# Two-layer RG-LRU and forgetting-attention trunk: splits of y later and spread, low parts of weights on VectorE, single banks for the end blocks

## The chip, the core and the metric

The kernel runs on one core of a Trainium2 chip. A core has five engines that each work through their own queue in order: TensorE (PE in the profile, with its weight loads as PEld), VectorE (DVE), ScalarE (ACT), GpSimd (POOL) and SyncE (SP), which here issues the DMA transfers. The metric is the time of one execution on the device in microseconds.

## The reference, cut to what matters

One batch of 1024 tokens by 1024 channels, two layers, float32. Layer 1 in the list is a recurrence; layer 2 is causal attention with 16 heads of 64, a forget gate in the logits, and a SiLU gate on its output.

```python
def fox_mixer(h, w_in, b_f, w_out):
    u = h @ w_in                                  # q, k, v, gate, forget logits
    cum = jnp.cumsum(jax.nn.log_sigmoid(f_logit), axis=1)
    # for each block of 128 queries:
    logits = jnp.einsum("bqhd,bkhd->bhqk", q_blk, kf) * scale
    logits = logits + (cq_blk[..., :, None] - ck[:, :, None, :])
    logits = jnp.where(mask[None, None], logits, NEG_INF)
    p = jax.nn.softmax(logits, axis=-1)
    o = jnp.einsum("bhqk,bkhd->bqhd", p, vf)
    y = o * jax.nn.silu(gate)
    return y @ w_out

def reference(x, ...):
    for i in range(DEPTH):                        # 2
        h = rms_norm(x, norm_g[i])
        x = x + (lru_mixer if i % 2 == 0 else fox_mixer)(h, ...)
    return rms_norm(x, final_g)
```

## The kernel before

Every float32 operand of a matmul is split into a high part, cast by ScalarE (`to_hi`), and a low part, the operand less the high one (`to_lo`). A product is three matmuls: high by high, high by low, low by high. For weights, `split_weights` loads `wf`, casts `wh` on the engine `hi_eng` and subtracts `wl` on `lo_eng`; `weights` does so for four (or fewer) 128x128 blocks at a time.

The first layer fills the time to about 440 us, the second the rest. In the second, x is held transposed, channels on the partitions, in two halves `c` of 512 tokens, with the residual in DRAM (`x1d`). Heads go in pairs. For a head, `maxima` makes the scores S of each 128 queries, masks them and finds their maxima on VectorE and takes the exponentials p (and their sums) on ScalarE; `weigh` transposes p on TensorE, splits it into `ph` and `pl` and multiplies by the values into O, which goes to `yo`. At the end of a head's `maxima` the sums are turned to reciprocals, transposed on TensorE (`tr`), copied (`rc`) and sent through DRAM (`recd`, `recb`) so that they lie along the rows. `scale` multiplies the gate `sg` by `recb` on GpSimd, `gated` multiplies `yo` by that, also on GpSimd. For pairs 0 to 5 the result goes to DRAM (`y1d`); for pairs 6 and 7 `split_y` splits it into `yhh` and `yhl`, which stay in SBUF.

`run` walks a string of digits and dots: a digit advances a step of the attention, a dot takes one step of the generator `fill`, which gives TensorE work between. Up to head 11, `fill` projects the next pair's keys and queries (`kq_units`) and gate (`g_units`). From head 12 on it also holds `load_y` and `split_loaded` (y of pairs 0 to 5, six splits for each half), `partial` (the output projection over those six pairs, for blocks `db` of 128 channels and both halves, added to `x1d`) and `turned` for the first half. `turned` is an end block: it transposes the residual x into PSUM, adds the products of pairs 6 and 7, squares for the norm's sum (ScalarE) and multiplies by the norm's gains (`res`, VectorE). After the last head the first half's four results are scaled and stored, and `turned` runs for the second half. The values of four heads are projected by `values(g)`, g = 0 to 3.

The program's text doesn't set the order of each engine's queue alone: a scheduler that simulates the program's time line reorders instructions. `issue_after` ties a step to the matmul before it.

Of the kernel before, what the change touches and what calls it, by code (L numbers as in the profile page):

```python
# [38 lines left out]
def trunk(ctx: ExitStack, tc: tile.TileContext, xt, w0, wg, wo0, pc, gn, gf, w1, wv, wf, bf, wo1, out):  # L39
# [431 lines left out]
    with ExitStack() as l1:  # L471
# [30 lines left out]
        def values(g):  # L502
# [3 lines left out]
            for k in range(0, KT, 2):  # L506
                src = [(wv[g, :, k : k + 2], slice(0, 256))]
                if ex:
                    src.append((wf[:, k : k + 2], slice(256, 256 + ex)))
                parts += split_weights(src, (2, 256 + ex), nc.scalar, nc.gpsimd)  # L510
            Vs[2 * g], Vs[2 * g + 1] = [], []
# [32 lines left out]
        kqw = {}  # L544

        def kq_units(pair, parts=((1, (0, 1)), (0, (0, 1)))):

            for is_k, hs in parts:
# [4 lines left out]
                if hs[0] == 0 or pair == 0:  # L553
                    kqw[is_k] = list(weights(w1[is_k * 8 + pair]))
                hi, lo = kq[pair, is_k]
# [70 lines left out]
        first = values(0)  # L626
        for _ in range(9):
            next(first)
# [5 lines left out]
        def g_units(pair, hs=(0, 1)):  # L634

            if hs[0] == 0:
                sgs[pair] = at.tile([P, SEQ], F32, tag="sg", name="sg1")
                gw[0] = list(weights(w1[16 + pair]))
            sg = sgs[pair]

            def use(h, pt):
                g_ = sg[:, h * HALF : (h + 1) * HALF]
                nc.scalar.activation(g_, pt, AF.Tanh, scale=0.5)
                nc.vector.scalar_tensor_tensor(g_, g_, 1.0, pt, ALU.add, ALU.mult)

            yield from project(gw[0], use, hs)
# [107 lines left out]
        def gated(hd, c, sub=slice(0, HALF)):  # L754

            if hd % 2 == 0:
                return
            pair = hd // 2
            yo = yos[pair, c][:, sub]
            nc.gpsimd.tensor_tensor(  # L760
                yo, yo, sgs[pair][:, c * HALF + sub.start : c * HALF + sub.stop], ALU.mult
            )
            if hd >= 13:
                split_y(c, pair, yo, sub)
            else:
                nc.sync.dma_start(y1d[c, pair], yo)
# [47 lines left out]

# [11 lines left out]
        def residual(c, q):  # L826
            xs = [wpool.tile([P, 2, 256], F32, tag=("wh", "wl")[q], name="x1") for d in range(4)]
            for d, x in enumerate(xs):
                nc.sync.dma_start(x, x1d[c, :, 2 * d : 2 * d + 2, q * 256 : (q + 1) * 256])
            return xs  # L830

        def turned(c, q):
# [11 lines left out]
            for b in range(2):  # L844
                cs = slice(q * 256 + b * P, q * 256 + (b + 1) * P)
                ss = ssq[c][:, 4 * q + 2 * b : 4 * q + 2 * b + 2]
                for h, hs in enumerate(halves):
                    if c == 1 and b == 1:
                        if h == 0:
                            two = two_banks("turn")  # L850
                        pt = two[:, h]
                    else:
                        pt = ps.tile([P, HALF], F32, tag="gO"[c * q], name="turn")

                    for i in range(4):
                        x = xs[2 * h + i // 2][:, i % 2, b * P : (b + 1) * P]
                        matmul(pt[:, i * P : (i + 1) * P], x, ident, start=i == 0, stop=False, is_transpose=True)
# [59 lines left out]
        for hd in range(HEADS):  # L917
            pair = hd // 2
            if hd % 2 == 0:
                if hd < 12:  # L920
                    fill = kq_units(pair + 1, ((1, (0, 1)), (0, (0,))))
                elif hd == 12:
                    rest = [(db, c) for db in range(2, KT) for c in range(2)]
                    fill = chain(
                        kq_units(7),
                        g_units(7, (0,)),
                        load_y(0),
                        g_units(7, (1,)),
                        load_y(1),
                        split_loaded(0),  # L930
                        partial([(0, 0), (1, 0)]),
                        split_loaded(1),
                        partial([(0, 1), (1, 1)] + rest),
                        turned(0, 0),
# [6 lines left out]
            if hd == HEADS - 1:  # L941
                break
            scale(hd)
            gated(hd, 0)
            side = late() if hd == 14 else iter(())
            run(second, weigh(hd, 1), maxima(hd + 1, 0), fill=fill, side=side)
            drain(side)
            gated(hd, 1)
            if hd < 12:
                drain(fill)  # L950
            if hd % 4 == 3 and hd < 12:
                drain(values(hd // 4 + 1))
            if hd + 2 < HEADS:
# [13 lines left out]
        for q in range(2):  # L967
            left[1, q] = residual(1, q)
        r = root_mean(ssq[0])
        for i, o in enumerate(first_half):  # L970
            nc.vector.tensor_scalar(o, o, r[:, i : i + 1], None, ALU.mult)
            nc.sync.dma_start(out[i], o)
        run("." * 18, fill=chain(turned(1, 0), turned(1, 1)))


# [57 lines left out]
```

## Time and profile before

| | |
|---|---|
| runs, us | 1153.79, 1154.62, 1159.84 (median 1154.62) |
| profiled execution, us | 1156.08 |
| its span, us | 1154.1 |
| mean granted TensorE clock | 0.992 |
| busy TensorE, VectorE, ScalarE, GpSimd, us | 1121.8, 723.0, 593.2, 230.1 |
| low parts of weights on GpSimd | 114 instructions, 166.2 us |

Times in the views are counted from the start of the span. A row of a timeline gives start, duration, engine (SPq is SyncE's queue issuing a transfer), line, operation and tiles, out<-in, and in brackets how long the engine was idle before and what released it. A row of the chain of waits gives start, duration and what ran. A row of the waits gives who waited for whom, the total, the number of times and the longest. A row of the windows gives the length, then for each of TensorE, its weight loads, VectorE, ScalarE and GpSimd the busy time and number of instructions, then the granted TensorE clock, the share of the DMA engines and GB/s.

### The profile page before, as it was taken

Reading aid. Unit: us, or ns where it says so; the run is one execution under the profiler, and the core shown is the slowest. Engines: PE = TensorE matmul, PEld = TensorE weight load, DVE = VectorE, ACT = ScalarE, POOL = GpSimd, SP = SyncE. Lnnn points to the kernel's source line nnn. Section 1 sums busy time; section 2 is a strip of 40 time slices with the busy share of each in tenths; the row PEclk is TensorE's granted clock in tenths of the full one; section 3 lists DMA queues with packets and bytes.
Section 4 is the critical chain, followed back from the end, with each engine's and each line's share of the span. In section 5 each row is a group of like instructions: output and inputs, shape, how many; then the busy total and the mean of one; then the engine's idle time right before and its main releaser. Section 6 shows DMA issues by size and latency. Waiting matters only on the chain.

```text
span 1154.1 us, 15825 instructions
## 1 busy us (share of the span) xinstructions
PE 1121.8 (97%) x5713; PEld 942.8 (82%) x5713; DVE 723.0 (63%) x1222; ACT 593.2 (51%) x1081; POOL 230.1 (20%) x159
## 2 busy tenths in 40 slices
PE   9999999999999999999999999999999999979996
PEld 7788888888888887978888988889888898858874
DVE  7589766777567789566665356663666535746644
ACT  8388345355553657455555355554555534534434
POOL 1212112211121102342222122222232221011010
PEclk9999999999999999999999999999999999989999
DMA  6111111111111124353434135241352512835444
GB/s 212 51 41 51 46 56 52 41 55 41 51 55 40 56 64 157 88 134 88 120 84 107 46 88 124 79 119 45 77 129 74 129 44 67 237 104 160 130 128 182
DMA packets 63637, 105.42 MB, mean 91 GB/s; under 512 B 9444, under 2 KB 24420, under 8 KB 63560
## 3 DMA queue, kind: packets, MB, share of 16 engines
q1 hardware_dynamic: 63560, 104.42, 31.6%
q8 instruction: 45, 0.74, 0.3%
q14 instruction: 32, 0.26, 0.1%
HBM read 63.30 MB, written 15.93 MB: 69 GB/s over the span
## 4 chain that ended last, share of the span: by engine, by line
PE 86%; DVE 4%; issue 3%; DMA 3%; POOL 2%; ACT 2%; SPq 0%; POOLq 0%; ACTq 0%; DVEq 0%
PE gps L54 31%; PE ops L54 16%; PE ups L54 11%; PE vps L54 6%; PE S L54 6%; PE O L54 5%; PE pt L58 5%; PE gate L54 3%; PE turn L54 2%; DMA recb<-recd 1%; POOL sg L705 1%; POOL wl L96 1%; DMA recd<-rc 1%; DVE sq L162 1%; DVE hl L238 1%
## 5 line engine op out<-in xcount | busy, mean ns | idle before, releaser
L96 POOL TENSOR_TENSOR wl<-wf,wh 128x512 fp32r<-128x512 f32 (+1 forms) x114 | 166.2, 1463 | 664.3 <-ACT wh L85 472.2
L54 PE MATMUL gps<-hh,wh 128*128 128x512 f32 x576 | 228.9, 398 | 0.2 <-DVE qkl L565 0.2
L54 PE MATMUL gps<-hh,wl 128*128 128x512 f32 x576 | 226.7, 394 | 0.1
L54 PE MATMUL gps<-hl,wh 128*128 128x512 f32 x576 | 226.7, 393 | 0.0
L678 ACT ACTIVATE p<-S,m 128x128 f32<-128x128 f32 (+7 forms) x128 | 94.8, 741 | 141.1 <-DVE m L673 139.7
L85 ACT CAST wh<-wf 128x512 fp32r<-128x512 f32 (+2 forms) x156 | 94.4, 607 | 141.1 <-PE ops L54 41.9
L96 DVE TENSOR_TENSOR pl<-pt,ph 128x512 fp32r<-128x512 f32 (+1 forms) x198 | 98.8, 541 | 101.6 <-ACT ph L85 101.1
L54 PEld LDWEIGHTS gps<-hl,wh 128*128 128x128 f32 x576 | 108.2, 188 | 24.5
L54 PEld LDWEIGHTS gps<-hh,wl 128*128 128x128 f32 x576 | 108.7, 189 | 20.4 <-POOL wl L96 0.6
L54 PEld LDWEIGHTS gps<-hh,wh 128*128 128x128 f32 x576 | 108.5, 188 | 20.0 <-DVE qkl L565 0.4
L673 DVE CUSTOM_DVE_ANT_0 S<-S,mask 128x128 f32<-128x128 f32 (+7 forms) x128 | 97.4, 762 | 40.5 <-PE S L54 39.0
L85 ACT CAST ph<-pt 128x512 fp32r<-128x512 f32 (+1 forms) x198 | 83.0, 474 | 28.9 <-PE pt L58 23.5
L54 PE MATMUL S<-T,U 96*128 96x512 f32 (+7 forms) x384 | 92.1, 349 | 0.0
L361 DVE TENSOR_TENSOR x<-x,ops 128x512 f32<-128x512 f32 x80 | 54.1, 682 | 50.9 <-PE ops L54 50.8
L58 PE MATMUL pt<-ident,p 128*128 128x128 f32 x576 | 80.0, 275 | 0.0
L54 PEld LDWEIGHTS S<-T,U 128*128 128x128 f32 (+1 forms) x384 | 69.1, 190 | 13.2 <-ACT p L678 0.8
L54 PE MATMUL ups<-hh,wh 128*128 128x512 f32 x192 | 76.7, 400 | 2.5 <-DVE us L271 1.9
L58 PEld LDWEIGHTS pt<-ident,p 128*128 128x128 f32 x576 | 69.2, 142 | 10.7 <-issue 0.4
L54 PE MATMUL ups<-hl,wh 128*128 128x512 f32 x192 | 76.5, 398 | 0.2
L54 PE MATMUL ops<-yh,wh 128*128 128x512 f32 x192 | 76.1, 396 | 0.5 <-DVE x L453 0.5
L54 PE MATMUL vps<-wl,hh 128*128 128x256 f32 (+1 forms) x256 | 72.8, 286 | 3.7 <-POOL wl L96 3.7
L54 PE MATMUL ups<-hh,wl 128*128 128x512 f32 x192 | 76.0, 396 | 0.0
(176 smaller groups left out, 2184.3 us busy)
## 6 DMA issues: line engine op xcount, KB each, us to landing
wf<-in_w SPq DMA_DIRECT2D x100, 256.0 KB
wf<-in_wo SPq DMA_DIRECT2D x64, 128.0 KB
U<-qkh SPq DMA_DIRECT2D x64, 128.0 KB
T<-qkh SPq DMA_DIRECT2D x28, 256.0 KB
x<-in_xt SPq DMA_DIRECT2D x16, 256.0 KB
x1d<-x SPq DMA_DIRECT2D x16, 256.0 KB
wf<-in_wv SPq DMA_DIRECT2D x16, 256.0 KB
U<-qkl SPq DMA_DIRECT2D x32, 128.0 KB
```

What stands on the lines that cost most here:

```text
L54: pe[0] = nc.tensor.matmul(*args, **kw)
L58: pe[0] = nc.tensor.transpose(*args)
L85: nc.scalar.copy(hi, src)
L96: return eng.tensor_tensor(lo, src, f32(hi), ALU.subtract)
L162: eng.tensor_tensor(parts[0], parts[0], sq, ALU.add)
L238: nc.vector.scalar_tensor_tensor(lo, x, g_, f32(hi), ALU.mult, ALU.subtract)
L361: nc.vector.tensor_tensor(x, x, pt, ALU.add)
L673: nc.vector.tensor_tensor_reduce(S[:, :n], S[:, :n], mask[:, SEQ - n :], -1.0, -NEG, ALU.add, ALU.min, accum_out=m)
L678: seen[0] = nc.scalar.activation(p, S[:, :n], AF.Exp, bias=m, scale=-1.0, accum_out=sums[:, i : i + 1])
L705: nc.gpsimd.tensor_tensor(sg, sg, recs[hd // 2][rows, cs], ALU.mult)
```

## The change

Six things are edited.

1. `values` takes its low parts on VectorE for g = 1 to 3 (g = 0, which also carries the forget logits' columns, keeps GpSimd), and after its first two weight tiles it yields; the main loop takes that first step ahead of the second `run` of the head before.
2. `kq_units` and `g_units` of pairs 1 to 7 take their low parts on VectorE; pair 0 stays on GpSimd.
3. The split of y for pair 6 is called later in the program: half 0 after head 13's second `run`, half 1 after head 14's first, and no longer within `gated`.
4. `split_loaded` yields after every second pair, and `beside` takes its steps between steps of the gate projection and of `partial`, where they came as six at once. The weights of `partial` are split a block ahead (`split_out`).
5. `partial` goes two channel blocks at a time for each half. `residual` for the first quarter loads eight tiles of one block each; the others load as before, with the two tags exchanged.
6. `turned` takes one PSUM bank for each block of results, and the first half's four scalings and stores come from a generator, `finish`, that runs beside the last end blocks.

```diff
@@ values
-                parts += split_weights(src, (2, 256 + ex), nc.scalar, nc.gpsimd)
+                parts += split_weights(src, (2, 256 + ex), nc.scalar, nc.gpsimd if ex else nc.vector)
+                if k == 2:
+                    yield
@@ kq_units, g_units
+        def low(pair):
+            return nc.vector if pair else nc.gpsimd
...
-                    kqw[is_k] = list(weights(w1[is_k * 8 + pair]))
+                    kqw[is_k] = list(weights(w1[is_k * 8 + pair], lo_eng=low(pair)))
...
-                gw[0] = list(weights(w1[16 + pair]))
+                gw[0] = list(weights(w1[16 + pair], lo_eng=low(pair)))
@@ gated
-            if hd >= 13:
+            if hd == 15:
                 split_y(c, pair, yo, sub)
-            else:
+            elif hd < 13:
                 nc.sync.dma_start(y1d[c, pair], yo)
@@ split_loaded, partial
                 to_lo(yl, f32(yl), yh, nc.vector)
+                if pair % 2:
+                    yield
+
+        def beside(steps, first, more):
+
+            for i, _ in enumerate(steps):
+                if i >= first:
+                    next(more, None)
+                yield
+
+        def split_out(db):
+            if db < KT and db not in wo:
+                wo[db] = list(weights(wo1[db, :, :6], lo_eng=nc.vector))
+
+        def first_out():
+            split_out(0)
             yield from ()
...
-                if db not in wo:
-                    wo[db] = list(weights(wo1[db, :, :6], lo_eng=nc.vector))
+                split_out(db)
+                if c:
+                    split_out(db + 1)
@@ residual
-            xs = [wpool.tile([P, 2, 256], F32, tag=("wh", "wl")[q], name="x1") for d in range(4)]
+
+            cs = slice(q * 256, (q + 1) * 256)
+            if c == q == 0:
+                xs = [vpool.tile([P, 256], F32, tag=f"v{d}", name="x1", bufs=2) for d in range(KT)]
+                for d, x in enumerate(xs):
+                    nc.sync.dma_start(x, x1d[c, :, d, cs])
+                return xs
+            xs = [wpool.tile([P, 2, 256], F32, tag=("wl", "wh")[q], name="x1") for d in range(4)]
@@ turned
-                    if c == 1 and b == 1:
-                        if h == 0:
-                            two = two_banks("turn")
-                        pt = two[:, h]
-                    else:
-                        pt = ps.tile([P, HALF], F32, tag="gO"[c * q], name="turn")
+                    pt = ps.tile([P, HALF], F32, tag="gO"[c * b], name="turn")
@@ main loop, from head 12
-                    rest = [(db, c) for db in range(2, KT) for c in range(2)]
+                    pairs = ((0, 1), (2, 3), (4, 5), (6, 7))
+                    todo = [(db, c) for two in pairs for c in range(2) for db in two]
+                    splits = [split_loaded(c) for c in range(2)]
                     fill = chain(
                         kq_units(7),
                         g_units(7, (0,)),
                         load_y(0),
-                        g_units(7, (1,)),
+                        first_out(),
+                        beside(g_units(7, (1,)), 2, splits[0]),
                         load_y(1),
-                        split_loaded(0),
-                        partial([(0, 0), (1, 0)]),
-                        split_loaded(1),
-                        partial([(0, 1), (1, 1)] + rest),
+                        beside(beside(partial(todo), 0, splits[0]), 4, splits[1]),
                         turned(0, 0),
                         turned(0, 1),
                     )
@@ main loop, every head
+            if hd == 14:
+                split_y(1, 6, yos[6, 1])
             scale(hd)
             gated(hd, 0)
             side = late() if hd == 14 else iter(())
+            if hd % 4 == 3 and hd < 12:
+
+                vals = values(hd // 4 + 1)
+                next(vals)
             run(second, weigh(hd, 1), maxima(hd + 1, 0), fill=fill, side=side)
             drain(side)
             gated(hd, 1)
+            if hd == 13:
+                split_y(0, 6, yos[6, 0])
@@ after the last head
-        r = root_mean(ssq[0])
-        for i, o in enumerate(first_half):
-            nc.vector.tensor_scalar(o, o, r[:, i : i + 1], None, ALU.mult)
-            nc.sync.dma_start(out[i], o)
-        run("." * 18, fill=chain(turned(1, 0), turned(1, 1)))
+        def finish():
+
+            r = root_mean(ssq[0])
+            yield
+            for i, o in enumerate(first_half):
+                nc.vector.tensor_scalar(o, o, r[:, i : i + 1], None, ALU.mult)
+                nc.sync.dma_start(out[i], o)
+                yield
+                yield
+
+        run("." * 18, fill=chain(turned(1, 0), turned(1, 1)), side=finish())
```

How the change moves instructions on the engines, at three places. First, ScalarE around the split of y for pair 6, half 0 (`yhh<-yo`); `yhh<-yhl` are the high parts of the loaded y, `p<-S` an exponential, `ph<-pt` the high part of transposed p. Before:

```order
L678 ACTIVATE p,sums<-S,m 128x256
L85 CAST yhh<-yo 128x512
L85 CAST yhh<-yhl 128x512 x6
L85 CAST ph<-pt 128x512 x2
L85 CAST wh<-wf 128x512
L85 CAST wh<-wf 128x256
L678 ACTIVATE p,sums<-S,m 128x384
```

And now, in the same place:

```order
L683 ACTIVATE p,sums<-S,m 128x256
L85 CAST ph<-pt 128x512 x2
L85 CAST wh<-wf 128x512
L85 CAST wh<-wf 128x256
L85 CAST yhh<-yo 128x512
L683 ACTIVATE p,sums<-S,m 128x384
```

The six casts of loaded y have gone from here (they stand earlier in the queue), and the cast of `yo` has moved behind four others.

Second, TensorE at the same time, where the transpose `tr` of head 13's sums stands. Before, among the products O of the last weights of a head:

```order
L54 MATMUL O<-ph,v_8646 128x256
L689 MATMUL tr<-ident,sums 8x128
L54 MATMUL O<-pl,v_8646 128x256
L54 MATMUL O<-ph,v_8677 128x128
L54 MATMUL O<-pl,v_8677 128x128
L54 MATMUL S<-T_3598,U 128x256 x2
```

And now, in the output projection that follows (`ops`, of the block of channels 1 and half 0):

```order
L54 MATMUL ops_9403<-yhh,wl 128x512
L694 MATMUL tr<-ident,sums 8x128
L54 MATMUL ops_9403<-yhl,wh 128x512
L54 MATMUL S<-T_3598,U 128x256 x2
L54 MATMUL ops_9483<-yhh,wh 128x512
```

The transpose stands behind all but one of that block's matmuls; head 14's has moved too, and the rest of TensorE's order is as it was.

Third, VectorE at the end, from the last end blocks of the first half to the first of the second. Before:

```order
L869 TENSOR_TENSOR res<-turn,grow 128x512
L885 TENSOR_TENSOR ssq_4035<-ssq_4035 128x4
L888 RECIPROCAL ssq_4035<-ssq_4035 128x4
L971 TENSOR_SCALAR res<-res,ssq_4035 128x1024 x4
L869 TENSOR_TENSOR res<-turn,grow 128x512
L885 TENSOR_TENSOR ssq_4036<-ssq_4036 128x1
```

And now:

```order
L893 TENSOR_TENSOR res<-turn,grow 128x512
L909 TENSOR_TENSOR ssq_4035<-ssq_4035 128x4
L912 RECIPROCAL ssq_4035<-ssq_4035 128x4
L1006 TENSOR_SCALAR res<-res,ssq_4035 128x1024 x4
L893 TENSOR_TENSOR res<-turn,grow 128x512
L909 TENSOR_TENSOR ssq_4036<-ssq_4036 128x1
```

Nothing moved here but the line numbers. On GpSimd 54 subtractions `wl<-wf,wh` have gone, and VectorE has 54 more.

More of the change, by code (lines that the diff above doesn't have):

```diff
@@ L626, in trunk @@
         first = values(0)
-        for _ in range(9):
+        for _ in range(10):
             next(first)
@@ L826, in residual @@
         def residual(c, q):
-            xs = [wpool.tile([P, 2, 256], F32, tag=("wh", "wl")[q], name="x1") for d in range(4)]
+            cs = slice(q * 256, (q + 1) * 256)
[5 more added lines that the diff above has]
+            xs = [wpool.tile([P, 2, 256], F32, tag=("wl", "wh")[q], name="x1") for d in range(4)]
             for d, x in enumerate(xs):
-                nc.sync.dma_start(x, x1d[c, :, 2 * d : 2 * d + 2, q * 256 : (q + 1) * 256])
-            return xs
+                nc.sync.dma_start(x, x1d[c, :, 2 * d : 2 * d + 2, cs])
+            return [x[:, i] for x in xs for i in range(2)]
         def turned(c, q):
@@ L847, in turned @@
                 for h, hs in enumerate(halves):
-                    if c == 1 and b == 1:
-                        if h == 0:
-                            two = two_banks("turn")
-                        pt = two[:, h]
-                    else:
-                        pt = ps.tile([P, HALF], F32, tag="gO"[c * q], name="turn")
+                    pt = ps.tile([P, HALF], F32, tag="gO"[c * b], name="turn")
                     for i in range(4):
-                        x = xs[2 * h + i // 2][:, i % 2, b * P : (b + 1) * P]
+                        x = xs[4 * h + i][:, b * P : (b + 1) * P]
                         matmul(pt[:, i * P : (i + 1) * P], x, ident, start=i == 0, stop=False, is_transpose=True)
@@ L951, in trunk @@
             if hd % 4 == 3 and hd < 12:
-                drain(values(hd // 4 + 1))
+                drain(vals)
             if hd + 2 < HEADS:
```

## The prediction, made before the result was known

> **What bounds the kernel now.** I read the page's busy times first, then TensorE's waits grouped by what ended them, then the chain of waits and windows of 5 us around the large ones.
>
> ```profile
> PE 1121.8 (97%) x5713; PEld 942.8 (82%) x5713; DVE 723.0 (63%) x1222; ACT 593.2 (51%) x1081; POOL 230.1 (20%) x159
> PE ops L54 <- ACT yhh L85: 8.9, 1, 8.9
> PE turn L54 <- DVE res L869: 4.6, 2, 2.7
> PE vps L54 <- POOL wl L96: 3.7, 4, 1.1
> PE turn L54 <- DMA x<-x1d: 1.9, 1, 1.9
> ```
>
> TensorE is busy for 1121.8 of 1154.1 us. Its matmuls are the same before and after, in the same order but for two 8x128 transposes, so only the 32.3 us of idle time and stretches at a lower clock can be gained. Four waits hold 19.1 of those 32.3 us (8.9 + 4.6 + 3.7 + 1.9), and the change bears on each. The profiled execution took 1156.08 us. The sum is made against that; the runs' median, 1154.62, is 1.46 lower, and I take this off at the end.
>
> **Part A, values' low parts.** The matmuls of `values` wait for a low part made on GpSimd.
>
> ```profile
> 639.89 1.28 POOL L96 TENSOR_TENSOR wl<-wf,wh 128x512 fp32r<-128x512 f32 x1 [6.30 <-ACT wh L85]
> 641.23 0.39 PE L54 MATMUL vps<-wl,hh 128*128 128x256 f32 x1 [0.86 <-POOL wl L96]
> L96 DVE TENSOR_TENSOR wl<-wf,wh 128x512 fp32r<-128x512 f32 x34 | 23.2, 685 | 7.5 <-ACT wh L85 7.5
> ```
>
> VectorE now makes it for three of the four groups. GpSimd needs 1.28 us, VectorE 0.685 for the same shape. So each of three sites gains about 0.6 of a wait like this 0.86, **1.8 us** in all. The high parts' casts keep their place on ScalarE. Bounds: 0, if VectorE comes late to it, and 2.5, the three waits whole (3.7 less the fourth's 1.1).
>
> **Part B, the split of y for pair 6.** This is the large one.
>
> ```profile
> 1005.18 0.28 DVE L691 COPY rc<-tr 8x128 f32<-8x128 f32 x1 [0.54 <-PE tr L689]
> 1006.29 0.60 SPq L587 DMA_DIRECT2D U<-qkl  x1
> 1006.98 2.37 DMA recd<-rc
> 1009.37 4.08 DMA recb<-recd
> 1013.59 2.33 POOL sg L705
> 1016.00 1.27 POOL yo L760
> 1017.30 1.15 ACT yhh L85 x2
> 1018.49 0.79 PE L54 MATMUL ops<-yhh,wh 128*128 128x512 f32 x1 [8.85 <-ACT yhh L85]
> 1015.00:1020.00 5.00, 1.51 (x4) 1.11 (x5) 2.05 (x4) 2.70 (x6) 2.19 (x2) 0.50 0.12 45
> 1020.00:1025.00 5.00, 5.00 (x23) 4.16 (x22) 3.22 (x6) 2.11 (x4) 0.00 (x0) 0.76 0.00 0
> ```
>
> The softmax sums of head 13 go through DRAM (recd, recb), GpSimd scales the gate and then y, and only then can ScalarE cast y. Behind that cast, in ScalarE's queue, stand six casts of loaded y that need nothing from it; TensorE waits for the first of them, 8.85 us. The clock is then low: 1.51 us of work at 0.50 in the first window and 5.00 at 0.76 in the second give 1.51 x 0.50 + 5.00 x 0.24 = 1.95 us. Together 10.8 us.
>
> In the changed order the six casts stand earlier, and between TensorE and the late cast lies only what stands behind it: the exponentials of 384 columns (p384), which free the scores' buffer that the next 128x512 scores need.
>
> ```profile
> 1008.99 0.40 PE L54 MATMUL ops<-yhl,wh 128*128 128x512 f32 x1
> 1022.83 0.93 PE O L54 x4
> 1023.76 2.79 PE ops L54 x12
> 1028.29 0.76 PE pt L58 x7
> 1029.98 0.47 PE S L54 x2
> 1027.84 0.58 ACT L678 ACTIVATE p<-S,m 128x384 f32<-128x384 f32 x1 [0.85 <-DVE m L673]
> 533.17 0.26 SPq L692 DMA_DIRECT2D recd<-rc  x1
> 534.39 0.48 SPq L696 DMA_DIRECT2D recb<-recd  x1
> ```
>
> Without the wait TensorE wants those scores at 1009.64 (1018.49 - 8.85) + 3.19 (what now runs from there to 1023.76, at full clock: six ops, half of 2.79, then eight transposes, 8/7 of 0.76, then four products, 0.93) + 6.22 (1029.98 - 1023.76) = 1019.05. The transpose of the sums now stands ahead of the matmul at 1008.99 and no longer ahead of the copy at 1005.18, some 4.1 us later; so the copy ends at about 1009.6. From the issue of recd to that of recb it takes between 1.2 us (533.17 to 534.39, with SyncE hardly loaded) and 2.4 (here); from there to GpSimd 4.2 (1009.37 to 1013.59), to ScalarE 3.7 (to 1017.30), then 0.6 for the cast and 0.6 for p384. The buffer is free at 1019.9 to 1021.1, a wait of 0.9 to 2.1 us. I take the middle: **a new wait of 1.5 us** in place of 8.85, and 0.5 for a short loss of clock (it is 1.7 or nothing, as part C shows). In SyncE's changed queue an x1d write stands between the two issues, of a block whose products are done by 1009.64; I add nothing for it. Gain 10.8 - 2.0 = **8.8 us**, bounds 7.0 (wait 2.1 and clock 1.7) and 10.8 (transfers quick enough for no wait).
>
> A row of part C shows the half clock after an idle time of only 1.92 us, while the 2.66 us before 1136.57 (part D) cost no clock at all: that window has 1.00. The Trainium skill ("TensorE: Matmul & The Clock Gate", Part 1) tells of a free-running window of about 3.4 us and has as its short rule to leave no idle gap above that. By this rule the new wait would cost no clock and the sum would be 0.5 better; the row at 1.92 us disagrees with the short form of the rule, and the measurement decides.
>
> **Part C, the load of the residual.**
>
> ```profile
> 1095.53 0.41 SPq L820 DMA_DIRECT2D x1d<-xp  x1
> 1101.56 0.33 SPq L820 DMA_DIRECT2D x1d<-xp  x1
> 1104.14 2.27 SPq L829 DMA_DIRECT2D x<-x1d  x4
> 1105.98 4.44 DMA x<-x1d
> 1110.00:1115.00 5.00, 4.53 (x18) 3.75 (x19) 0.97 (x3) 1.34 (x4) 0.00 (x0) 0.66 0.05 18
> 1135.00:1140.00 5.00, 3.43 (x19) 2.87 (x20) 2.58 (x8) 2.00 (x5) 0.00 (x0) 1.00 1.02 398
> ```
>
> The first end block waits 1.9 us for the last piece of x, which lands at 1110.42, 4.4 us after its issue in a batch of four, and then runs at a lower clock: 5.00 x 0.34 = 1.7. Changed, (7,0) is finished before (6,1), so its write moves from 1101.56 to the slot at 1095.53, and the eight loads go out one by one, each behind its write. The last is issued about 1101 and lands at 1105.5, where TensorE wants it at 1108.5. Gain 1.9 + 1.7 = **3.6 us**. The bounds are 1.9 (the clock is lost anyhow) and 3.6; a cover of 3 us is what hides the load.
>
> **Part D, the end.**
>
> ```profile
> 1124.71 3.72 PE turn L54 x20
> 1131.91 2.74 DVE L971 TENSOR_SCALAR res<-res,ssq 128x1024 f32<-128x1024 f32 x4
> 1135.83 0.68 DVE L869 TENSOR_TENSOR res<-turn,grow 128x512 f32<-128x512 f32 x1
> 1136.57 0.66 PE L54 MATMUL turn<-ident,x 128*128 128x128 f32 x4 [2.66 <-DVE res L869]
> 1146.14 0.66 PE L54 MATMUL turn<-ident,x 128*128 128x128 f32 x4 [1.93 <-DVE res L869]
> 1149.82 0.72 ACT L873 ACTIVATE res<-res,ssq 128x512 f32<-128x512 f32 x1 [0.38 <-DVE ssq L888]
> ```
>
> A tile of two banks holds the two halves of the second row block, so the second half waits until VectorE has read the first, behind four scalings of 2.74 us. With a bank for each half that wait goes. VectorE's order stays as it is: the four scalings still stand in one block, whatever the text of the change says, so nothing is priced for them. What is late next: two end blocks take 3.72 us and end at 1128.43, so the fifth of the eight that follow would start at 1128.43 + 4 x 1.86 = 1135.87. It needs a bank that VectorE now reads between the scalings' end (1131.91 + 2.74 = 1134.65) and 1135.3, one product of 0.68: 0.6 us to spare. The eight then end at 1143.3 instead of 1148.2 (1146.14 and a block of some 2.0), and the last scaling on ScalarE starts that much before 1149.82. That is 4.9 by the chain and 4.6 by the two waits; I take **4.7 us**. Bounds: 2.3, if half comes back behind the scalings (they then run 2.4 later than I place them, and the spare 0.6 is gone), and 5.1. After the last scaling stand the same stores as now.
>
> **Part E, what is added.** 54 low parts (42 of layer 2's keys, queries and gates, 12 of values') go from GpSimd to VectorE: 54 x 0.685 = 37 us more on an engine with 431 us idle.
>
> ```profile
> 612.10 0.62 ACT L85 CAST wh<-wf 128x512 fp32r<-128x512 f32 x1 [0.36 <-PE gps L54]
> 615.02 1.10 DVE L673 CUSTOM_DVE_ANT_0 S<-S,mask 128x896 f32<-128x896 f32 x1 [1.16 <-PE S L54]
> ```
>
> At a typical site ScalarE ends the cast at 612.7, VectorE is in the masking of scores until 613.8 and then idle for 1.16 us, until TensorE's next scores. The subtraction of 0.69 fits there, so I cost it **nothing**; without such a gap it is 0.685 each, on the way from scores to exponentials. Two other effects come for free: a weight's low part comes 0.6 us sooner, and GpSimd's gate scaling isn't queued behind it. The bound above is thus 0, the bound below 37.
>
> **Sum.** 1.8 + 8.8 + 3.6 + 4.7 = 18.9; 1156.08 - 18.9 = 1137.2; less 1.46 gives 1135.7, so **1136 us**. With all lower bounds of A to D the gain is 11.2 (1143.4), with all upper ones 22.0 (1132.6).
>
> **Rivals.** (1) The hand-off of pair 6 still holds ScalarE: recd goes out as late after its copy as now (1006.98 for a copy done at 1005.46, with loads of U ahead of it, the last at 1006.29), so everything is 1.5 later than the upper figure above, TensorE waits 3.6 us and loses 1.7 of clock. For it: SyncE's queue works in order and is as full there. Against it: the loads of U stood in front at 1005, not at 1009.6. The gain of B is 5.5, the time 1139.
>
> (2) The end doesn't do what it says: scalings in one block, and a bank freed no earlier than now, so D gives nothing: 1140.4. Against it: the two waits name the half of the same tile.
>
> (3) VectorE's queue becomes the bound. It works in order, so a moved subtraction that waits for its ScalarE cast holds the masking of scores behind it, that holds the exponentials, and TensorE stands. For it: the cast itself waits for TensorE to leave a weight buffer (0.36 at 612.10), and the order on VectorE is fixed. If each of the 54 costs 0.1 to 0.3, the time is 1141 to 1152. At 18.9 / 54 = 0.35 us each nothing is left, and above that the kernel is slower; with 0.685 each it is 1135.7 + 37 = 1172.7. Against it: the gap of 1.16 us, and TensorE runs scores ahead by two buffers.
>
> **How the numbers follow.** The forecast has 0.64, rival 1 0.15, rival 2 0.07, rival 3 below its turning point 0.09 and above it 0.05. The forecast's own range is 1132.5 to 1139. To leave out no more than 2 in 10, the range takes in rivals 1 and 2 and the lower bounds: **1131 to 1144**. A measurement of this kernel can tell about 0.5%, or 5.8 us, from no change. Faster by more than that (below 1148.8) are the forecast, rivals 1 and 2 and most of rival 3's first part: 0.91. Within it lies the rest of that part and the neighbourhood of the turning point: 0.04; slower: 0.05.
>
> **What would show it.** In the profile after: no TensorE wait for yhh, and a wait of 0.9 to 2.1 us on p at the scores of 512 columns near 1019 (B); the waits for res and for x from x1d gone, the clock at 1.00 where it was 0.66 (C, D); vps waits for VectorE of some 0.3 us three times (A); VectorE busy about 760 us and GpSimd about 151 (230.1 less 54 of its 1.46 us), with TensorE waiting no longer on S or p between 450 and 950 us than now (E). The prediction is wrong if TensorE's idle time comes out above 20 us: the waits would then have moved, not gone.

## The result, and the profile after

The changed kernel takes 1138.53 us (median of 4 runs, 1138.24 to 1139.6) against 1154.49 (1153.79 to 1159.84) for the kernel before: the ratio is 0.9854, with a 95% interval from 0.9823 to 0.9884. In a second comparison, which the experiments on the values share, it was 0.9849 (0.983 to 0.9868). Forecast were 1136 us and a range from 1131 to 1144. The profiled execution took 1138.24 us, with a span of 1136.5.

The page's busy times and TensorE's waits of the changed kernel:

```profile
PE 1116.5 (98%) x5713; PEld 937.5 (82%) x5713; DVE 757.9 (67%) x1276; ACT 592.1 (52%) x1081; POOL 163.5 (14%) x105
PE ups L54 <- ACT hh L87: 2.4, 2, 1.2
PE vps L54 <- DVE sg L649: 2.1, 3, 0.7
PE S L54 <- ACT p L683: 2.0, 2, 1.2
PE vps L54 <- ACT wh L85: 0.9, 3, 0.3
PE vps L54 <- POOL wl L96: 0.8, 1, 0.8
PE vps L54 <- DVE wl L96: 0.7, 3, 0.2
```

The span is 17.6 us shorter (1154.1 - 1136.5). TensorE's idle time fell from 32.3 to 20.0 us, which is 12.3 of it; its busy time fell by 5.3 with the same 5713 instructions, and nearly all of that is clock. Taken over windows of 5 us (busy time times what the clock lacks of 1.00), the profile of before loses 5.1 us, that of after 0.1. Of the 5.1 us, 1.5 were lost at 50 us, where the change edits nothing.

The waits for yhh (8.9), for res (4.6) and for x (1.9) are gone. New are one for p, one for sg, and 2.0 us more for hh, which lies in the first 12 us of the program, where the change moves nothing; over the profiles of this study it comes out between 0.4 and 2.4 us.

First the place of the hand-off, in the changed kernel's time lines of SyncE, GpSimd, VectorE, ScalarE and TensorE:

```profile
1009.74 0.28 SPq L697 DMA_DIRECT2D recd<-rc  x1
1011.38 0.47 SPq L701 DMA_DIRECT2D recb<-recd  x1
1015.15 2.39 POOL L710 TENSOR_TENSOR sg<-sg,recb 64x1024 f32<-64x1024 f32 x1 [39.82 <-DMA recb<-recd]
1015.16 2.94 DVE L96 TENSOR_TENSOR wl<-wf,wh 128x512 fp32r<-128x512 f32 x1 [0.53 <-ACT wh L85]
1018.62 0.55 DVE L678 CUSTOM_DVE_ANT_0 S<-S,mask 128x384 f32<-128x384 f32 x1
1019.29 0.62 ACT L85 CAST yhh<-yo 128x512 fp32r<-128x512 f32 x1 [2.98 <-POOL yo L765]
1019.81 0.57 ACT L683 ACTIVATE p<-S,m 128x384 f32<-128x384 f32 x1
1020.53 0.73 PE L54 MATMUL S<-T,U 128*128 128x512 f32 x2 [1.23 <-ACT p L683]
1015.00:1020.00 5.00, 4.30 (x23) 3.33 (x21) 4.44 (x6) 1.24 (x4) 4.03 (x2) 1.00 0.32 110
```

TensorE waits 1.23 us at the scores of 512 columns, due at 1019.30; the clock stays at 1.00. One row was in no one's sum: VectorE's subtraction at 1015.16 takes 2.94 us in place of 0.69, beside GpSimd's product that begins at 1015.15.

Then the end, in the chain of waits and VectorE's time line:

```profile
1112.07 18.55 PE turn L54 x100
1119.28 2.74 DVE L1006 TENSOR_SCALAR res<-res,ssq 128x1024 f32<-128x1024 f32 x4
```

Ten end blocks run without a gap (18.55 us, 1.86 each) past the four scalings, which still stand in one block.

### The profile page after: what moved, and what is told of

Same layout as the page of the kernel before. It is cut to its first block, busy times and chain, and to the rows that moved or that the text cites. A ratio compares the mean times of both kernels' runs of the same rounds, so it can differ in the third digit from the quotient of the medians.

```text
span 1136.5 us, 15822 instructions
## 1 busy us (share of the span) xinstructions
PE 1116.5 (98%) x5713; PEld 937.5 (82%) x5713; DVE 757.9 (67%) x1276; ACT 592.1 (52%) x1081; POOL 163.5 (14%) x105
## 4 chain that ended last, share of the span: by engine, by line
PE 89%; DVE 3%; ACT 2%; issue 2%; DMA 2%; POOL 1%; SPq 0%; POOLq 0%; ACTq 0%; DVEq 0%
PE gps L54 33%; PE ops L54 15%; PE ups L54 11%; PE vps L54 7%; PE S L54 6%; PE O L54 6%; PE pt L58 5%; PE turn L54 3%; PE gate L54 2%; DVE sq L162 1%; POOL wl L96 1%; DMA x<-in_xt 1%; DVE wl L96 0%; DVE x L453 0%; DMA wf<-in_wo 0%
## 5 line engine op out<-in xcount | busy, mean ns | idle before, releaser
L96 POOL TENSOR_TENSOR wl<-wf,wh 128x512 fp32r<-128x512 f32 (+1 forms) x60 | 98.1, 1639 | 395.9 <-ACT wh L85 342.8
L710 POOL TENSOR_TENSOR sg<-sg,recb 64x1024 f32<-64x1024 f32 (+1 forms) x17 | 39.2, 2306 | 460.2 <-DMA recb<-recd 444.6
L96 DVE TENSOR_TENSOR wl<-wf,wh 128x512 fp32r<-128x512 f32 x96 | 72.1, 756 | 26.0 <-ACT wh L85 25.3
L58 PEld LDWEIGHTS pt<-ident,p 128*128 128x128 f32 x576 | 67.4, 140 | 12.4 <-issue 2.2
L54 PE MATMUL vps<-wh,hh 128*128 128x256 f32 (+1 forms) x256 | 73.7, 288 | 3.0 <-DVE sg L649 2.1
```

The costliest lines, as they stand in the source:

```text
L54: pe[0] = nc.tensor.matmul(*args, **kw)
L58: pe[0] = nc.tensor.transpose(*args)
L96: return eng.tensor_tensor(lo, src, f32(hi), ALU.subtract)
L710: nc.gpsimd.tensor_tensor(sg, sg, recs[hd // 2][rows, cs], ALU.mult)
```

## The experiments

**The low parts alone.** The kernel before with edits 1 and 2.

```diff
-                parts += split_weights(src, (2, 256 + ex), nc.scalar, nc.gpsimd)
+                parts += split_weights(src, (2, 256 + ex), nc.scalar, nc.gpsimd if ex else nc.vector)
+                if k == 2:
+                    yield
...
+        def low(pair):
+            return nc.vector if pair else nc.gpsimd
...
-                gw[0] = list(weights(w1[16 + pair]))
+                gw[0] = list(weights(w1[16 + pair], lo_eng=low(pair)))
```

> The kernel before with edits 1 and 2 alone (54 low parts from GpSimd to VectorE, the first two weight tiles of values a step ahead). Theory: the profile after shows that TensorE's wait for GpSimd's wl at the three groups of values (0.9 each) is only exchanged for one of 0.7 for sg, which VectorE now reaches one subtraction later, and 0.2 for wl; elsewhere VectorE's idle time takes the subtractions. So the time is that of the kernel before within 1 us (1153.5 to 1155.5). Rival 1, step A of the prediction: 1.8 us faster. Rival 2, the subtractions stand in the way of the masking of scores: slower by 2 us or more, with TensorE waiting for p or S between 500 and 950 us.

1158.49 us against 1155.04: ratio 1.0028 (1.0012 to 1.0043), so 3.2 us slower, which neither the theory nor step A had. Its waits between 500 and 950 us are those of the changed kernel, and TensorE reaches the last group of values at the same time as before (947.2 and 947.4 us); rival 2's waits for p or S aren't there. The profiled span is 2.3 us longer, and the windows near its end show where:

```profile
1135.00:1140.00 5.00, 4.15 (x16) 3.47 (x17) 1.86 (x6) 1.71 (x4) 0.00 (x0) 0.68 0.89 347
1145.00:1150.00 5.00, 3.11 (x11) 2.47 (x10) 1.04 (x2) 1.16 (x3) 0.00 (x0) 0.71 0.28 105
```

At the same two waits for res that the kernel before has (2.58 and 1.89 us here) the clock went low this time: 4.15 x 0.32 + 3.11 x 0.29 = 2.2 us. That isn't the whole account, though. By the same windows this profile loses 5.5 us of clock over its whole span and that of the kernel before 5.1, since the kernel before lost 1.5 us each near 50 and 1110 us, where this one lost nothing. So the two profiles don't show that the clock makes the difference; the last experiment asks it in another way.

**The splits of y alone.** The kernel before with edit 3 and the spreading of edit 4.

```diff
-            if hd >= 13:
+            if hd == 15:
                 split_y(c, pair, yo, sub)
-            else:
+            elif hd < 13:
...
                 to_lo(yl, f32(yl), yh, nc.vector)
+                if pair % 2:
+                    yield
...
```

> The kernel before with edit 3 and the spreading of edit 4 alone; the order of blocks in the output projection, the end blocks and the engines of low parts stay. Theory: the wait of 8.85 us for yhh and the 1.95 us of lost clock go, and a wait of 1.2 us for p at scores of 512 columns comes, as in the profile after: 9 to 10 us faster, about 1145. Rival: part of the gain of the changed kernel there comes from the other edits, and this alone gives under 7 us.

1145.01 us, ratio 0.9917 (0.9893 to 0.994): 9.6 us faster (6.9 to 12.4). Its waits:

```profile
PE turn L54 <- DVE res L877: 4.6, 2, 2.7
PE vps L54 <- POOL wl L96: 2.5, 3, 0.9
PE S L54 <- ACT p L678: 2.1, 2, 1.5
```

The wait for yhh is gone, the one for p has come, and those for res and for GpSimd's wl stay nearly as before (the latter 2.5 in place of 3.7). The theory holds.

**The late call undone.** The changed kernel with edit 3 taken back; the casts stay spread in the program's text.

```diff
-            if hd == 15:
+            if hd >= 13:
                 split_y(c, pair, yo, sub)
-            elif hd < 13:
+            else:
...
-            if hd == 14:
-                split_y(1, 6, yos[6, 1])
...
-            if hd == 13:
-                split_y(0, 6, yos[6, 0])
```

> The changed kernel with edit 3 undone: split_y of pair 6 stands in gated again, the six casts of loaded y stay spread in the program's text. Theory: where the late cast is called decides. ScalarE's queue has the cast of yo ahead of the six casts of the second half again, and with it the wait for yhh of 8 to 9 us and the lower clock: 9 to 10 us slower than the changed kernel, about 1148. Rival: the spreading alone does it, and the time stays within 1 us of 1138.5.

1147.19 us, ratio 0.993 (0.991 to 0.995), so 8.8 us slower than the changed kernel by the two ratios (0.0076 of 1154.5). ScalarE's and TensorE's time lines:

```profile
1016.59 0.62 ACT L85 CAST yhh<-yo 128x512 fp32r<-128x512 f32 x1 [5.70 <-POOL yo L765]
1017.11 3.21 ACT L85 CAST yhh<-yhl 128x512 fp32r<-128x512 f32 x6
1017.78 0.79 PE L54 MATMUL ops<-yhh,wh 128*128 128x512 f32 x1 [8.38 <-ACT yhh L85]
```

The six casts stand behind the late one again. Spreading the casts in the program's text alone leaves the wait nearly as it was (8.38 us for 8.85), so the later call is needed. Whether the later call would do it without the spreading wasn't run.

**The cast in another queue.** The kernel before, with the split of pair 6's y on GpSimd.

```diff
             if hd >= 13:
-                split_y(c, pair, yo, sub)
+                e = dict(hi=nc.gpsimd, lo=nc.gpsimd) if hd < 15 else {}
+                split_y(c, pair, yo, sub, **e)
...
```

> The kernel before with one edit: the split of pair 6's y on GpSimd, high and low part. Theory: TensorE's wait for yhh came from ScalarE's queue alone, so taking the late cast out of that queue does what edits 3 and 4 do: the wait of 8.9 us goes with the lost clock, 9 to 11 us faster, 1144 to 1146. Rival: TensorE needs the split y itself soon after, and most of the wait stays.

1149.33 us, ratio 0.9951 (0.9926 to 0.9976): 5.7 us faster, about half of what was expected. TensorE's wait for yhh falls from 8.85 to 2.04 us, which is what the first of the six casts is late by:

```profile
1011.60 0.62 PE L54 MATMUL ops<-yhh,wh 128*128 128x512 f32 x1 [2.04 <-ACT yhh L85]
1011.58 7.39 DVE L96 TENSOR_TENSOR yhl<-yhl,yhh 128x512 fp32r<-128x512 f32 x6 [1.14 <-ACT yhh L85]
```

They no longer stand behind the late cast, but still just ahead of their use. VectorE's six low parts took 7.39 us beside GpSimd's work, where they had taken 3.70 in the kernel before. By the two profiles TensorE's idle time falls by 6.8 us (32.3 to 25.5), its busy time not at all (1121.8 and 1121.6): the clock is low in other windows here (0.66 at 925 us, 0.68 at 1010 us, 0.76 at 1105 us), so the gain of clock that the expectation counted on didn't come.

**The banks alone.** The kernel before with one bank for each block of `turned`; no `finish`.

```diff
-                    if c == 1 and b == 1:
-                        if h == 0:
-                            two = two_banks("turn")
-                        pt = two[:, h]
-                    else:
-                        pt = ps.tile([P, HALF], F32, tag="gO"[c * q], name="turn")
+                    pt = ps.tile([P, HALF], F32, tag="gO"[c * b], name="turn")
```

> The kernel before with only the single banks of edit 6 (turned takes one bank for each block); the four scalings are left as they were. Theory: the two waits for res at the end go (2.66 and 1.93), 4.5 to 5 us faster, about 1149.7, and VectorE still does the four scalings in one block. Rival: without the generator finish the scalings hold the fifth block, and only about half, 2.3 us, is gained.

1149.83 us, ratio 0.9948 (0.9932 to 0.9965): 6.0 us faster (4.0 to 7.9). Its chain has the same ten blocks without a gap as the changed kernel:

```profile
1125.73 18.55 PE turn L54 x100
```

So the banks give it, and the generator for the scalings isn't needed; it leaves VectorE's order as it was.

**The order of the output projection undone.** The changed kernel with the blocks in the old order and four loads in place of eight for the first quarter.

```diff
-                    todo = [(db, c) for two in pairs for c in range(2) for db in two]
+                    todo = [(0, 0), (1, 0), (0, 1), (1, 1)] + [(db, c) for db in range(2, KT) for c in range(2)]
...
-            if c == q == 0:
+            if False:
```

> The changed kernel with edit 5 undone as far as the first quarter goes: the output projection's blocks in the order of the kernel before, and its residual loaded in four pieces. Theory: the wait for x from x1d (1.6 to 2.5 us) comes back at the first end block, 2 us slower than the changed kernel, and 1.7 more where the clock goes low behind it: 1140.4 to 1142.3. Rival: with the earlier splits of y the load is in time anyhow, 1138.5.

1140.27 us, ratio 0.9851 (0.9808 to 0.9895), which can't be told from the changed kernel. The profile shows the wait back, and the clock at 1.00 behind it:

```profile
PE turn L54 <- DMA x<-x1d: 1.6, 1, 1.6
1100.00:1105.00 5.00, 3.93 (x26) 3.39 (x27) 2.48 (x5) 1.73 (x5) 0.24 (x1) 1.00 0.28 99
```

The span can't be used for the price: it is 1138.1 for 1136.4 in the changed kernel's second profile, but 1.7 us of clock were lost at 50 us here and none there, and the idle time is the same (19.4 and 19.5). The end itself shows it: from the start of the first end block to that of the seventh 16.72 us pass here (1096.82 to 1113.54), 14.92 in the changed kernel (1096.99 to 1111.91). So the edit is worth 1.8 us there, the wait with its restart. The clock loss behind the wait comes in some executions and not in others: six profiles of this study have the wait, and three of them lose 1.3 to 1.5 us behind it.

**A free bank for the values.** The changed kernel; the second of eight results goes to the scores' tag.

```diff
-                if ex and st % 2:
+                if (ex and st % 2) or st == 1:
```

> The changed kernel again, beside the next three on the same chip: 1138 to 1139.

> The changed kernel with one edit: the second of the eight results of a group of values takes a bank of the scores' tag S and no longer the bank that sg is still read from. Theory: the three waits of TensorE for sg (0.7 each) go and nothing takes their place, so 2.1 us faster than the changed kernel, 1136.4. Rival: another wait behind it is late too (VectorE's parts of the values, or the scores' buffer), and the gain is under 0.7 us.

The changed kernel took 1139.5 us here, this one 1131.51 (1131.07 to 1132.46), ratio to before 0.9779 (0.976 to 0.9798): 8.0 us faster than the changed kernel where 2.1 were expected (6.7 by the spans of the two profiles, 1136.4 and 1129.7). What waits at the first of the three groups in the changed kernel, in the time lines of VectorE and TensorE:

```profile
638.62 0.69 DVE L96 TENSOR_TENSOR wl<-wf,wh 128x512 fp32r<-128x512 f32 x1
639.34 0.69 DVE L756 TENSOR_TENSOR yo<-yo,O 64x512 f32<-64x512 f32 x1
640.07 0.69 DVE L649 SCALAR_TENSOR_TENSOR sg<-sg,gps 128x512 f32<-128x512 f32 x1
638.64 0.39 PE L54 MATMUL vps<-wh,hh 128*128 128x256 f32 x1 [0.30 <-ACT wh L85]
639.37 0.39 PE L54 MATMUL vps<-wl,hh 128*128 128x256 f32 x1 [0.22 <-DVE wl L96]
639.83 0.28 PE L54 MATMUL vps<-wl,hh 128*128 128x256 f32 x1
640.81 0.39 PE L54 MATMUL vps<-wh,hh 128*128 128x256 f32 x1 [0.70 <-DVE sg L649]
```

The second result needs the bank from which VectorE has yet to read the gate (sg), and that reading stands behind yo. The moved subtraction isn't what makes it late: it fills a gap in which VectorE was idle in the kernel before (0.60 us ahead of yo). From VectorE's scaling of gps (639.15 before, 637.97 changed) to the start of sg it is 2.02 us before and 2.10 in the changed kernel. In the kernel before, the reading and the second result's first matmul stood like this:

```profile
641.17 0.69 DVE L644 SCALAR_TENSOR_TENSOR sg<-sg,gps 128x512 f32<-128x512 f32 x1
641.92 0.38 PE L54 MATMUL vps<-wh,hh 128*128 128x256 f32 x1
```

The reading ends at 641.86 and the matmul starts 0.06 later, so the bank was already the next bound, and TensorE's wait for GpSimd's low part hid it. With another bank the scheduler also puts the first products of both results ahead of the last products O, so all three waits go, not one. And a wait costs more than its idle time: from 639.83 to 640.81 pass 0.98 us where two such matmuls otherwise start 0.12 apart, a loss of 0.86 for 0.70 shown. Counted in this way over all three waits of the group (from the last product O at 638.06 to the second matmul behind the last wait at 641.03, eight starts of 0.12), the loss is 2.0 us where 1.2 are shown. The groups of one kind of these matmuls (durations, first and last start), changed kernel and this one:

```profile
L54 PE MATMUL vps<-wh,hl x256: 279/282/372, 463.8 to 947.5; 128*128 128x256 f32 x96, 128*128 128x272 f32 x32
```

```profile
L54 PE MATMUL vps<-wh,hl x256: 279/282/372, 463.4 to 940.0; 128*128 128x256 f32 x96, 128*128 128x272 f32 x32
```

From first to last it is 483.7 against 476.6 us: 7.1 for three groups, of which the waits that the view shows are 3.7; at 2.0 for each group the waits and their restarts make 6.0, and the last 1.1 isn't taken apart.

**The split of pair 6 on GpSimd in the changed kernel, and both together.**

```diff
...
-                split_y(1, 6, yos[6, 1])
+                split_y(1, 6, yos[6, 1], hi=nc.gpsimd, lo=nc.gpsimd)
...
-                split_y(0, 6, yos[6, 0])
+                split_y(0, 6, yos[6, 0], hi=nc.gpsimd, lo=nc.gpsimd)
```

> The changed kernel with the split of pair 6's y (both halves, high and low part) on GpSimd, which makes that y, in place of ScalarE and VectorE. Theory: the wait of 1.2 us for p at the 512-column scores was ScalarE standing at the late cast, so it goes, and the other one for p of 0.8 us too: 2 us faster than the changed kernel, 1136.5. Rival: the wait was set by VectorE's subtraction that took 2.9 us in place of 0.7 beside GpSimd and held the masking of the scores behind it; then the wait stays at 0.5 us or more.

> The edits of the two runs before together: 4.1 us faster than the changed kernel, 1134.4, if both theories hold; with either rival some 1136.5, with both 1138.5.

The first gives 1137.13 us, ratio 0.9828 (0.9808 to 0.9847): 2.4 us faster than the changed kernel beside it, as the theory had it, with intervals that touch. Its waits for p fall to 0.8, the longest 0.5, so the rival has its part too: p of 384 columns is now held by the masking, that by the long subtraction.

```profile
1016.66 2.58 DVE L96 TENSOR_TENSOR wl<-wf,wh 128x512 fp32r<-128x512 f32 x1 [0.54 <-ACT wh L85]
1020.41 0.58 ACT L683 ACTIVATE p<-S,m 128x384 f32<-128x384 f32 x1 [2.59 <-DVE m L678]
```

Both edits together give 1131.8 us, ratio 0.9779 (0.9759 to 0.9799): no different from the bank alone. With the bank's edit on top, the changed kernel takes 1131.51 us, the least of this study beside the run with both.

**VectorE beside GpSimd.** A measurement behind the changed kernel's last work.

```diff
+        for _ in range(14):
+            nc.gpsimd.tensor_tensor(g3, g1, g2, ALU.mult)
+        probe()   # VectorE: 4 x s1 - s2, 4 x pt - s2 (pt in PSUM), 4 copies
+        nc.vector.tensor_copy(s1, g3)
+        probe()
```

> The changed kernel with a measurement put behind its last work: VectorE does four subtractions of 128x512 with both operands in SBUF, four with one operand in PSUM, and four copies from SBUF, first while GpSimd multiplies 128x512 tiles in SBUF 14 times without pause, then the same alone. Theory: a subtraction with both operands in SBUF is held while GpSimd works (1.3 us or more each against 0.69 alone), one with an operand in PSUM isn't (0.69 both times). Rival: each of them is slowed by the same share, or none, and the 2.9 us seen in the changed kernel came from something else.

The end's own work got between the probe's parts, and the four subtractions from PSUM came only after GpSimd was done; the end's products `turn` by `grow`, which also read PSUM, stand in for them. GpSimd's and VectorE's time lines:

```profile
1122.28 21.13 POOL L1031 TENSOR_TENSOR g<-g,g 128x512 f32<-128x512 f32 x14
1134.45 0.68 DVE L893 TENSOR_TENSOR res<-turn,grow 128x512 f32<-128x512 f32 x1
1135.05 0.88 DVE L898 TENSOR_SCALAR res<-res,ssq 128x512 f32<-128x512 f32 x1
1135.86 1.75 DVE L1024 TENSOR_TENSOR dd<-s,s 128x512 f32<-128x512 f32 x1
1137.53 1.21 DVE L909 TENSOR_TENSOR ssq<-ssq 128x1 f32<-128x1 f32 x1
1149.48 2.86 DVE L1024 TENSOR_TENSOR dd<-s,s 128x512 f32<-128x512 f32 x4
```

Alone four subtractions in SBUF take 2.86 us, 0.71 each; beside GpSimd single ones take 1.35 to 1.75. One of a single column takes 1.21, where such a row takes 0.16 in the changed kernel; three others there take 0.09 to 0.62. The product with an operand in PSUM keeps its 0.68. The theory holds for subtractions with both operands in SBUF. The subtractions from PSUM and the copies weren't seen beside GpSimd.

**All low parts back on GpSimd.** The changed kernel without edits 1 and 2 as far as engines go.

```diff
...
-            return nc.vector if pair else nc.gpsimd
+            return nc.gpsimd
```

> The changed kernel with all 54 low parts back on GpSimd. Edits 1 and 2 alone had made the kernel before 3.2 us slower, while its profile showed no dearer wait, only more time at a low clock late in the span. Theory: the 54 subtractions cost and bring nothing, the waits for values are exchanged one for one, and the 3.2 us were clock lost behind waits that the changed kernel no longer has: 1138 to 1139.5 here. Rival 1: the subtractions on VectorE cost 3 us of themselves, then this is faster than the changed kernel, 1135 to 1136. Rival 2, step A of the prediction: 1.8 us slower, 1140 to 1141.

1138.41 us (1137.49 to 1139.39), ratio 0.9848 (0.9834 to 0.9861): that of the changed kernel (0.9854 and 0.9849 in its two comparisons). Moving 54 subtractions brought nothing and cost nothing that these runs can tell. TensorE waits for GpSimd's low parts again, and no longer for sg:

```profile
PE vps L54 <- POOL wl L96: 2.6, 3, 0.9
50.00:55.00 5.00, 5.00 (x17) 3.94 (x16) 3.83 (x4) 2.35 (x3) 0.07 (x1) 0.66 0.18 52
```

The second row is the window behind the wait at 50 us, which the last section takes up. So the 3.2 us of the first experiment aren't the price of the subtractions in the changed kernel. That they were clock lost behind waits which the changed kernel doesn't have would agree with this, but the total of clock lost in the first experiment's profile (5.5 us for 5.1) doesn't bear it out, and its five runs (1155.99 to 1160.86) lie almost wholly above the eight beside them (1153.7 to 1156.79), for which chance alone is a poor account. Where those 3.2 us come from stays open.

## Why the prediction was right, point by point

The likeliest case came, 1138.53 for 1136. By the number alone rival 1 (1139) lies nearer; the traces decide between them. In the terms of the sum:

**B was right in its mechanism, nearly so in size.** The wait of 8.85 went, and the new one came at the place and in the form named, the 512-column scores behind p384, due at 1019.30 for 1019.05 forecast. It took 1.23 us for 1.5, and no clock was lost for the 0.5 taken. That is 10.8 - 1.2 = 9.6 in place of 8.8; the splits alone measured 9.6. Rival 1 fell: recd goes out at 1009.74, right behind the copy. What the working lacked was the second cause at that place, the subtraction beside GpSimd; with ScalarE's cast taken away, the wait fell only to 0.5.

**D was right.** 4.7 forecast, 4.6 by the waits that went and 6.0 (4.0 to 7.9) for the banks alone. VectorE's order with four scalings in one block did stand, and didn't matter. Rival 2 fell.

**C was right in its wait, and its clock was luck.** The 1.9 us are gone. The 1.7 us of clock that I added as certain (1.5 by that window's busy time of 4.53) are a loss that three of the six profiles with this wait show, the one I read among them; with the wait put back into the changed kernel, that execution lost none.

**A failed.** "So each of three sites gains about 0.6 of a wait like this 0.86": the wait for wl did fall by that, from 0.86 to 0.22, but TensorE then stood 0.70 us for the bank of the next result. VectorE's reading of the gate frees that bank, and it came when it always had: in the kernel before it ended at 641.86, and the matmul that needs the bank started at 641.92. The wait for wl had only covered it; the moved subtraction made the reading later by 0.08 us, no more. I asked what is late next at B and D and didn't ask it here; the bound of 0 was put to VectorE coming late to the subtraction, not to what was due right behind the wait. The three sites' waits were 3.5 before (wl and wh) and are 3.7 now, and 1.8 us of the forecast didn't come.

**E was right.** VectorE is busy for 757.9 us (about 760 forecast), and no wait on S or p appears between 450 and 950 us. GpSimd's 163.5 were put at 151, since I took its mean of 1.46, which holds slower ones of the first layer; the 54 that left took 66.6 / 54 = 1.23. Rival 3 fell: all low parts back gave the same time. Only the kernel before, with nothing but these low parts moved, was 3.2 us slower, and that stays unexplained.

**The rest of the miss** is in two places. The step "the runs' median, 1154.62, is 1.46 lower, and I take this off" assumed that the next profiled execution would stand to its median as this one did; it stood at 1138.24 below a median of 1138.53. That is 1.75 of the 2.8 us by which 1138.53 lies above the sum's 1135.7. The other 1.0 is the profiled execution itself (1138.24 for 1137.2): A's 1.8 and the waits for hh, 2.0 longer, against 0.8 more of B and the 1.5 us of clock at 50 to 55 us, which this execution by luck didn't lose. That adds up to 1.5, and the difference of 0.5 isn't taken apart. And TensorE's idle time ended at 20.0 us, on the very mark that I had set for a prediction gone wrong; the mark counted the exchange in the values and the start as moved waits, and rightly.

## What to carry to other kernels

When a cast waits for a long hand-off, look at what is queued behind it on its engine: here six casts that needed nothing from it cost 10 us, and placing the call later in the program, with the casts spread ahead of it, took nearly all of it away. Before pricing a shorter wait, look in the kernel as it stands for what comes free at the very end of that wait: here a bank came free 0.06 us before TensorE used it, and the 0.6 us taken from one wait returned as another of 0.7. And where PSUM tiles rotate through two banks, ask which bank the next result needs and who reads it last: a bank of its own gave 6 us at the end (4 to 8) and 8 us at the values.

## What the runs showed of the hardware that I had not expected

A short wait can cost twice. Behind the same wait of 1.9 us for VectorE's tile `us` at 49 us, the clock is low in some executions and full in others: of the 14 profiles of this study, seven have 0.66 to 0.75 in the window behind it and seven have 1.00. Windows of the kernel before and of the changed kernel:

```profile
50.00:55.00 5.00, 5.00 (x17) 3.98 (x16) 3.84 (x4) 2.34 (x3) 0.08 (x1) 0.70 0.16 52
```

```profile
50.00:55.00 5.00, 5.00 (x24) 4.08 (x23) 3.78 (x4) 2.62 (x3) 0.30 (x1) 1.00 0.16 56
```

The loss is up to 1.7 us where it comes. In the run with the banks alone it even followed waits of 0.35 and 0.86 us at the values (0.66 in the window from 640 us). The Trainium skill ("TensorE: Matmul & The Clock Gate", Part 1) has a free-running window of some 3.4 us, which agrees with the same wait being punished in one execution and not in another; its short rule, to have no idle gaps above that, would let these shorter waits pass, and the rows with 0.66 and 0.70 show a loss behind them all the same. It may also be why the kernel with fewer waits spreads less from run to run (1138.2 to 1139.6 against 1153.8 to 1159.8); that wasn't tested by itself.

VectorE's subtractions with both operands in SBUF are held while GpSimd works: 0.69 us becomes 1.35 to 2.94, and an addition of a single column took 1.21, while a product with one operand in PSUM kept its 0.68. The Trainium skill ("SBUF — State Buffer", Who interferes with whom) states that a VectorE instruction with two inputs in SBUF contends with a GpSimd instruction that reads SBUF, and that such contention is an exclusive lock. The row of 2.94 us agrees: it begins 0.01 us after GpSimd's product of 2.39 and ends 0.56 behind it. Low parts of weights are just this kind of operation, so in these rows a low part on VectorE is quick only where GpSimd is idle at that moment.
